# RWKV decay, rate and key scalings on ScalarE, and the last mLSTM block normalised on VectorE

## The chip, the cores and the metric

The kernel runs on one core of one Trainium2 chip. The metric is the device time of one execution in microseconds (us). Before the change it is 2755.69 us, the median of three runs (2754.13 to 2758.62 us). Engines are named as in the profile: PE is TensorE's matmuls, PEld its weight loads, DVE is VectorE, ACT is ScalarE, POOL is GpSimd, SP issues DMAs.

## What is computed

One layer over 4096 tokens of width 1024, batch 1, float32. One input projection feeds four mixers of width 256 (RWKV-7, multi-scale pooling, mLSTM, retention); each mixer's output is multiplied by a SiLU gate; the four are concatenated, projected, added to the residual and to a gated embedding, and layer-normalised. The parts that the change touches, cut from the reference:

```python
# RWKV: decay, rate and key
w_log = -jax.nn.softplus(-(w0 + jnp.tanh(wl) @ w2)) - 0.5
decay = jnp.exp(-jnp.exp(w_log))
a = jax.nn.sigmoid(a0 + al @ a2)
kk = normalised per head (k * k_k)
k = heads(k) * (1.0 + (a - 1.0) * k_a)
# state = state * decay + (state @ -kk) (kk * a)^T + v k^T ; y = state @ r
...
# mLSTM, at its end
h = num / jnp.maximum(jnp.abs(den), jnp.exp(-m_t))[..., None]
h = h * jax.nn.sigmoid(o_pre)
h = _head_norm(h, HEAD_NORM_EPS) * ln_w          # then times silu(gate)
```

`_head_norm` subtracts the mean over a head's 64 channels and divides by the standard deviation. The sigmoids are computed as tanh of half the argument, so that an affine step follows each tanh: for the decay it is `-0.5*exp(-0.5)*(t + 1)`, whose running sum over a chunk of 64 tokens goes into two exponentials; for the rate it is `-0.5*(t + 1)`; for the key it is `t * half[4+p] + half[6+p]`, a factor and an offset per channel.

## The kernel before, in words

The sequence is cut into 16 blocks of 256 tokens (`TB`, `NB`). The kernel runs in stages, one after the other over all blocks: pooling, retention, mLSTM (`_mlstm`), RWKV (`_rwkv_out`), and the output projection (`out`). Every float32 matmul of a projection is written as three matmuls on a high and a low part of its operands (`fetch`, lines 87 to 89: ACT casts the high part, DVE or POOL subtracts to get the low part).

The program is written for a scheduler that orders each engine's instructions ahead of time with its own timing model: an engine's queue is fixed when the program is built, and each engine then works through its queue in order. Instructions inside `self.soon()` have a higher priority there. In the RWKV stage the order of TensorE is written by hand: `mm` and `dense_k` keep program order, and the strings `START`, `THIRD` and `ORDER` say in which order pieces of the stages run (a name, a block offset, and how many eighths of a projection).

**RWKV, one block.** `la` projects the low-rank part. `k`, `r`, `v` and `g` project key, receptance, value and gate into one of two PSUM banks (`MM = 2`, tag `mm`); `mixed` (lines 1361 to 1373) empties a bank: for each half p, ACT multiplies (line 1369), then DVE adds the shifted part (line 1370). Stage `l` makes decay and rate: eight matmuls into `lw` and `lA`; ACT tanh into `tw` (line 319) and `ta` (line 320), each in two halves; the affine step of `tw` on DVE over 512 columns (line 321); two scans on DVE (line 323), one for each half; then ACT's two exponentials `E` (line 327) and `Ei` (line 328). Stage `n` normalises the key. Stage `m` makes the operands of the recurrence: `km` from `ta` on DVE, one instruction for each half (line 368), times `k` (line 370); `ta` scaled on DVE (line 371), then times `k` (line 375); products with `E` and `Ei` give `BK` (lines 378, 379) and `AR` (lines 382, 385). `inv` and `iv` invert 64x64 triangles with many small DVE instructions on `nt` and `xs` (lines 505, 514, 530), go through HBM and back into `X`, and `pt`, `px`, `pu`, `py` finish the inverse on PE.

**The chain of states.** `chain` runs twelve pieces for each block, at the letters C of the order: four chunks with three pieces each. In a chunk PE multiplies the state `S` by `AR` into `ry`; ACT copies `R` (line 636); PE makes `sa`; ACT copies `SAV` (line 643); PE makes `ds`; DVE updates the state in four instructions (line 660); ACT copies `Y` (line 666). The next chunk's first matmul needs the new state. Of the order of a steady block, the middle reads:

```python
"... C r.0/2 C l.0 r.0/3 C n.0 r.0/4 C vt.1 r.0 m.0 C g.0/4 ..."
```

**mLSTM's normalisation.** `mix(b)` ends with `head_norm` (line 711 on) on `Y` of 128 x 512. Statistics (lines 718, 720) and the added epsilon (line 722) are DVE's, the power -0.5 is POOL's (line 723). With `scaled=True`, as mLSTM calls it for all blocks, DVE then computes minus mean times `rs` (line 727) and ACT applies scale and offset, one instruction of 64 columns for each of 8 groups (line 729). With `scaled=False`, as retention and RWKV call it, DVE subtracts the mean (line 732), which doesn't need the power, and multiplies by `rs` (line 733), over 512 columns each. After either, DVE multiplies by the gate (line 1301) and SP stores the block.

The last mLSTM block and the start of RWKV overlap: `rwkv_first` has projected block 0's `la`, `k`, `r` and gate, and `START` goes on with `v#0/3 l#0 v#0 n#0 m#0 la#1 k#1/4 ...`.

Of the kernel before, what the change touches and what calls it, by code (L numbers as in the profile page):

```python
# [9 lines left out]
F32 = mybir.dt.float32  # L10
F32R = mybir.dt.float32r
AF = mybir.ActivationFunctionType
ALU = mybir.AluOpType
# [4 lines left out]
P = 128  # L18
# [22 lines left out]
DECAY = math.exp(-0.5)  # L41
HEAD_EPS = 1e-6
# [4 lines left out]
class Trunk:  # L47
# [148 lines left out]
    def _rwkv_out(self, es):  # L196
        nc, tc, a = self.nc, self.tc, self.a
        pool = lambda name, **kw: es.enter_context(tc.tile_pool(name=name, reuse_waits="tile", **kw))
        cp = pool("rc", bufs=1)
        p1 = pool("r1", bufs=1)  # L200
# [8 lines left out]
        V = nc.vector  # L209
        A = nc.scalar  # L210
        Q = nc.gpsimd
# [12 lines left out]
        smask = self.load(cp, "smask")  # L224
        lnw = self.load(cp, "rw_ln_w", a["rw_ln_w"].partition_broadcast(P))
        lnb = self.load(cp, "rw_ln_b", a["rw_ln_b"].partition_broadcast(P))
        half = cp.tile([P, 8], F32, name="rhalf", tag="rhalf")
        V.tensor_scalar(out=half[:, 0:4], in0=prm[:, 7:11], scalar1=0.5, scalar2=None, op0=ALU.mult)
        V.tensor_scalar(out=half[:, 4:6], in0=prm[:, 13:15], scalar1=0.5, scalar2=None, op0=ALU.mult)
        V.tensor_scalar(out=half[:, 6:8], in0=half[:, 4:6], scalar1=-1.0, scalar2=1.0, op0=ALU.mult, op1=ALU.add)  # L230
# [66 lines left out]
        @stage  # L297
        def l(b):

            la = bl[b]["la"]  # L300
            lah = p1.tile([P, 2, TB], F32R, name=f"lah{b}", tag="E")
            lal = p1.tile([P, 2, TB], F32R, name=f"lal{b}", tag="ta")
            lz = [wk.tile([P, 2, TB], F32, name=f"l{g}{b}", tag="wk") for g in range(2)]
            for g in range(2):
                own, other = slice(64 * g, 64 * g + 64), slice(64 - 64 * g, 128 - 64 * g)
                A.copy(out=lah[own, g], in_=la[own])
                A.copy(out=lah[other, g], in_=la[own])
                Q.memset(lal[other, g].bitcast(F32), 0.0)
                V.tensor_tensor(out=lal[own, g], in0=la[own], in1=lah[own, g].bitcast(F32), op=ALU.subtract)
            for g in range(2):  # L310
                for p in range(2):
                    mm(lz[g][:, p], LW[g][:, p], lah[:, g], start=(p == 0), stop=False, skip_group_check=True)
                for p in range(2):
                    mm(lz[g][:, p], LW[g][:, p], lal[:, g], start=False, stop=(p == 1), skip_group_check=True)
            lw, lA = lz
            tw = p1.tile([P, 2, TB], F32, name=f"tw{b}", tag="tw")
            ta = p1.tile([P, 2, TB], F32, name=f"ta{b}", tag="ta")
            for p in range(2):
                A.activation(out=tw[:, p], in_=lw[:, p], func=AF.Tanh, scale=0.5, bias=half[:, p:p + 1])
                A.activation(out=ta[:, p], in_=lA[:, p], func=AF.Tanh, scale=0.5, bias=half[:, 2 + p:3 + p])  # L320
            V.tensor_scalar(out=tw, in0=tw, scalar1=-0.5 * DECAY, scalar2=-0.5 * DECAY, op0=ALU.mult, op1=ALU.add)
            for p in range(2):
                V.tensor_tensor_scan(out=tw[:, p], data0=smask, data1=tw[:, p], initial=0.0, op0=ALU.mult, op1=ALU.add)
            E = p1.tile([P, 2, 4, 65], F32, name=f"E{b}", tag="E")
            Ei = t4(tw)
            Q.memset(E[:, :, :, 0:1], 1.0)
            A.activation(out=E[:, :, :, 1:], in_=Ei, func=AF.Exp)
            A.activation(out=Ei, in_=Ei, func=AF.Exp, scale=-1.0)
            eC = p2.tile([P, 2, 4], F32, name=f"eC{b}", tag="eC", bufs=3)
            Q.tensor_copy(out=eC, in_=E[:, :, :, 64])  # L330
            bl[b].update(ta=ta, E=E, Ei=Ei, eC=eC)
            yield 0.9
# [30 lines left out]
        @stage  # L363
        def m(b):
            k, r, ta, E, Ei = (bl[b][x] for x in ("k", "r", "ta", "E", "Ei"))
            km = p1.tile([P, 2, TB], F32, name=f"km{b}", tag="km")
            for p in range(2):
                V.tensor_scalar(out=km[:, p], in0=ta[:, p], scalar1=half[:, 4 + p:5 + p], scalar2=half[:, 6 + p:7 + p],
                                op0=ALU.mult, op1=ALU.add)
            V.tensor_tensor(out=km, in0=km, in1=k, op=ALU.mult)  # L370
            V.tensor_scalar(out=ta, in0=ta, scalar1=-0.5, scalar2=-0.5, op0=ALU.mult, op1=ALU.add)
            BK = p1.tile([P, 2, 2, 4, 64], F32, name=f"BK{b}", tag="BK")
            AR = [p4.tile([P, 2, 4, 64], F32, name=f"AR{b}_{cc}", tag="AR") for cc in range(2)]
            for p in range(2):
                V.scalar_tensor_tensor(out=ta[:, p], in0=k[:, p], scalar=prm[:, 11 + p:12 + p], in1=ta[:, p],
                                       op0=ALU.mult, op1=ALU.mult)
            for cc in range(2):
                V.tensor_tensor(out=BK[:, :, cc, 0::3], in0=c5(t4(km))[:, :, cc], in1=c5(Ei)[:, :, cc], op=ALU.mult)
                V.tensor_tensor(out=BK[:, :, cc, 1:3], in0=c5(t4(ta))[:, :, cc], in1=c5(Ei)[:, :, cc], op=ALU.mult)
            for cc in range(2):  # L380
                for p in range(2):
                    V.scalar_tensor_tensor(out=AR[cc][:, p, 1:3], in0=c5(t4(k))[:, p, cc],
                                           scalar=prm[:, 11 + p:12 + p], in1=c5(E[:, :, :, 0:64])[:, p, cc],
                                           op0=ALU.mult, op1=ALU.mult)
                V.tensor_tensor(out=AR[cc][:, :, 0::3], in0=c5(t4(r))[:, :, cc], in1=c5(E[:, :, :, 1:])[:, :, cc],
                                op=ALU.mult)
            rk = p1.tile([P, 2, TB], F32, name=f"rk{b}", tag="tw")
            Q.tensor_tensor(out=rk, in0=r, in1=km, op=ALU.mult)
            ST = [p4.tile([P, 2, 2, P], F32, name=f"ST{b}_{cc}", tag="ST") for cc in range(2)]
            g1 = [p4.tile([P, 2, 2, 2, P], F32, name=f"g1{b}_{cc}", tag="g1") for cc in range(2)]  # L390
            bl[b].update(rk=rk, BK=BK, AR=AR, ST=ST, g1=g1)
            return
            yield
# [296 lines left out]
        for i in range(self.NB + 2):  # L690
            gens = {}
            for w in ("" if i == 1 else START if i == 0 else THIRD if i == 2 else ORDER).split():
# [6 lines left out]
                nm, b = w.replace("#", ".").split(".")  # L699
                b = int(b) if "#" in w else i - int(b)  # L700
# [376 lines left out]
    def _mlstm(self, es):  # L1077
# [5 lines left out]
        cp = pool("mc", bufs=1)  # L1083
        self.mm = pool("mmm", bufs=3, space=PSUM)
        ident = self.ident
        V, A, Q = nc.vector, nc.scalar, nc.gpsimd
# [128 lines left out]
        def mix(b):  # L1215
# [28 lines left out]
            Y = p2.tile([P, 2, G], F32, name=f"Ym{b}", tag="Ym")  # L1244
            tot = p2.tile([P, 2, 4, 65], F32, name=f"tot{b}", tag="tot", bufs=1)
            for c in range(2):
# [40 lines left out]
                for i in range(4):  # L1287
# [9 lines left out]
                            in0=tot[:, :, :, 0:64].rearrange("p c h v -> p (c h) v"),  # L1297
                            in1=den.rearrange("p c h -> p (c h)").unsqueeze(2).broadcast_to([P, 8, 64]), op=ALU.mult)
            V.scalar_tensor_tensor(out=Y, in0=so, scalar=1.0, in1=Y, op0=ALU.add, op1=ALU.mult)
            self.head_norm(p1, Y, HEAD_EPS, f"m{b}", True)  # L1300
            V.scalar_tensor_tensor(out=Y, in0=Y, scalar=0.5, in1=sg, op0=ALU.mult, op1=ALU.mult)
            self.store(b, 2, Y)

# [2 lines left out]
        p1 = pool("m1", bufs=1)  # L1306
        p2 = pool("m2", bufs=2)
        wk = pool("mwk", bufs=1, space=PSUM)
        for i in range(1, self.NB + 1):
            if i < self.NB:  # L1310
                dense(i)
            mix(i - 1)
# [483 lines left out]
```

## Time and profile before

| | before |
|---|---|
| median of three runs | 2755.69 us |
| profiled execution, device time | 2756.33 us |
| profiled execution, span of the trace | 2754.5 us |
| mLSTM's last normalisation and RWKV's start | about 1207 to 1300 us of the span |
| RWKV, steady blocks | about 1300 to 1840 us |
| RWKV, last blocks, with the first embedding blocks | about 1840 to 2020 us |

The span is the time from the first to the last instruction in the profile; the 1.8 us between it and the execution's time lie around it. Times in the rows are counted from the start of the span. A matmul's busy time is modelled, and matmuls overlap in the pipeline, so a stretch in which PE is shown as fully busy can still hold short waits: those are read from the idle times, not from the share.

### The profile page before, as it was taken

The page shows a single profiled execution, that of the slowest core. Times are in us where ns is not written, and L with a number is a line of the kernel's source. Part 1 is how long each engine was busy: PE and PEld are TensorE (multiplying, and loading weights), DVE is VectorE, ACT ScalarE, POOL GpSimd, SP SyncE. Part 2 cuts the span into 40 slices and gives each one's busy share as a digit, 9 for nine tenths or more (in the row PEclk, how much of TensorE's full clock was granted, in tenths as well). Part 3 has the DMA queues.
Part 4 walks back from the last instruction along what each step waited for, and adds up shares of the span by engine and source line. Part 5 has one row for each costly group of instructions (what it writes and reads, how often), then busy time and mean ns, then how long its engine had stood idle before and what let it go on. Part 6 is the DMA issues. An engine that isn't in the chain of part 4 may idle for free.

```text
span 2754.5 us, 57727 instructions
## 1 busy us (share of the span) xinstructions
PE 2653.0 (96%) x21940; PEld 2382.7 (87%) x21940; DVE 2142.6 (78%) x5241; ACT 1111.2 (40%) x2700; POOL 1142.9 (41%) x1302
## 2 busy tenths in 40 slices
PE   8999999998999999989999999999989999899996
PEld 8998888878899999988999999998988888778885
DVE  6767888886887777777888888888564666789997
ACT  4323222334666666653444444445222333422221
POOL 4664555554433434431323333324243111266665
PEclk9999999999999999999999999999999999999998
DMA  5453222223311112231111111113366444734431
GB/s 170 146 174 113 59 61 66 66 69 95 99 55 58 55 55 65 74 107 34 53 39 51 39 51 39 51 40 110 117 197 220 135 140 145 237 123 156 157 138 69
DMA packets 251909, 270.66 MB, mean 98 GB/s; under 512 B 69616, under 2 KB 175344, under 8 KB 251632
## 3 DMA queue, kind: packets, MB, share of 16 engines
q1 hardware_dynamic: 251632, 266.98, 31.0%
q8 instruction: 172, 2.82, 0.4%
q14 instruction: 105, 0.86, 0.1%
HBM read 203.40 MB, written 63.50 MB: 97 GB/s over the span
## 4 chain that ended last, share of the span: by engine, by line
PE 40%; DVE 16%; DMA 7%; issue 4%; POOL 3%; ACT 2%; SPq 1%; POOLq 0%; DVEq 0%; ACTq 0%
PE ry L262 2%; DVE ro L1688 2%; PE zqk L150 2%; PE zqk L151 2%; PE zqk L149 2%; DVE nt L505 1%; DVE ro L1667 1%; DVE ro L1670 1%; PE zg L158 1%; DMA nd<-g 1%; POOL ro L1671 1%; PE zg L159 1%; PE zg L160 1%; DVE so L1662 1%; PE num L1265 1%
## 5 line engine op out<-in xcount | busy, mean ns | idle before, releaser
L1446 ACT CAST Ah<-xr 128x512 fp32r<-128x512 f32 x189 | 117.0, 620 | 280.7 <-PE zrb L1482 55.3
L1447 DVE TENSOR_TENSOR Al<-xr,Ah 128x512 fp32r<-128x512 f32 x135 | 95.6, 710 | 80.6 <-ACT Ah L1446 77.2
L150 PE MATMUL zqk<-xl,wh_w_ml 128*128 128x256 f32 x512 | 150.6, 294 | 0.8 <-DVE xl L1126 0.8
L149 PE MATMUL zqk<-xh,wh_w_ml 128*128 128x256 f32 x512 | 149.8, 293 | 1.5 <-ACT xh L1125 1.2
L88 ACT CAST xh<-rawx 128x512 fp32r<-128x512 f32 x148 | 91.5, 619 | 146.4 <-DMA rawx<-in_xT 65.9
L151 PE MATMUL zqk<-xh,wl_w_ml 128*128 128x256 f32 x512 | 148.5, 290 | 0.0
L89 DVE TENSOR_TENSOR xl<-rawx,xh 128x512 fp32r<-128x512 f32 x148 | 116.0, 784 | 28.5 <-ACT xh L88 27.5
L677 POOL TENSOR_TENSOR SAV<-SAV,bon 64x256 f32<-64x256 f32 x64 | 42.9, 671 | 227.2 <-PE ry L262 226.1
L1447 POOL TENSOR_TENSOR Al<-xr,Ah 128x512 fp32r<-128x512 f32 x54 | 71.0, 1314 | 139.7 <-ACT Ah L1446 75.3
L1671 POOL TENSOR_TENSOR ro<-ro,ln_b 128x512 f32<-128x512 f32 x64 | 100.7, 1593 | 53.9 <-DVE ro L1670 53.9
L912 POOL TENSOR_TENSOR rot<-rot,sw 128x256 f32<-128x256 f32 x64 | 69.2, 1082 | 95.4 <-DVE sw L911 89.5
L149 PEld LDWEIGHTS zqk<-xh,wh_w_ml 128*128 128x128 f32 x512 | 99.1, 194 | 3.2 <-ACT xh L1125 1.5
L150 PEld LDWEIGHTS zqk<-xl,wh_w_ml 128*128 128x128 f32 x512 | 99.4, 194 | 2.9 <-DVE xl L1126 1.0
L151 PEld LDWEIGHTS zqk<-xh,wl_w_ml 128*128 128x128 f32 x512 | 99.3, 194 | 0.8
L1466 POOL TENSOR_TENSOR xr<-xr,xr 128x512 f32<-128x512 f32 x27 | 35.6, 1317 | 143.0 <-DVE xr L1463 132.7
L660 DVE SCALAR_TENSOR_TENSOR S<-ds,eC,Se 64x64 f32<-64x64 f32 x256 | 72.4, 283 | 22.0 <-PE ds L262 17.0
L1237 DVE SCALAR_TENSOR_TENSOR xc<-zc,c_convw,xc 128x256 f32<-128x256 f32 x192 | 83.3, 485 | 0.4
L437 DVE SCALAR_TENSOR_TENSOR g<-gp,rc,c_rmask 128x128 f32<-128x128 f32 x256 | 69.0, 341 | 18.3 <-PE gp L262 17.2
L149 PE MATMUL zu<-xh,wh_w_pl 128*128 128x256 f32 x256 | 74.8, 292 | 6.1 <-ACT wh_w_pl L88 6.1
L657 POOL TENSOR_TENSOR Se<-S,eC 64x128 f32<-64x128 f32 x128 | 59.2, 463 | 48.8 <-DVE S L660 44.0
L150 PE MATMUL zu<-xl,wh_w_pl 128*128 128x256 f32 x256 | 73.8, 288 | 3.9 <-DVE xl L89 3.9
L1446 ACT CAST Aho<-s 128x512 fp32r<-128x512 f32 x48 | 29.7, 621 | 115.3 <-PE zob L1482 52.4
(1130 smaller groups left out, 10570.2 us busy)
## 6 DMA issues: line engine op xcount, KB each, us to landing
rawx<-in_xT SPq DMA_DIRECT2D x148, 256.0 KB, 3.2
xr<-in_xT SPq DMA_DIRECT2D x108, 256.0 KB, 2.9
mr<-in_xT SPq DMA_DIRECT2D x64, 256.0 KB, 3.1
rp<-in_x SPq DMA_DIRECT2D x64, 256.0 KB, 3.0
s<-rp SPq DMA_DIRECT2D x64, 256.0 KB, 2.7
yo<-y SPq DMA_DIRECT2D x16, 1024.0 KB, 4.9
ro<-s SPq DMA_DIRECT2D x16, 1024.0 KB, 5.0
out<-ro SPq DMA_DIRECT2D x32, 512.0 KB, 2.6
```

The costliest lines, as they stand in the source:

```text
L88: nc.scalar.copy(out=hi, in_=raw)
L89: eng.tensor_tensor(out=lo, in0=raw, in1=hi.bitcast(F32), op=ALU.subtract)
L149: nc.tensor.matmul(out, lh(k), rh(k), start=(k == 0 and (apart or i == 0)), stop=False, skip_group_check=True)
L150: nc.tensor.matmul(out, lh(k), rl(k), start=False, stop=False, skip_group_check=True)
L151: nc.tensor.matmul(out, ll(k), rh(k), start=False, stop=(k == nk - 1), skip_group_check=True)
L437: V.scalar_tensor_tensor(out=g1[cc][:, hh, p, e], in0=gp[hh][:, p, e], scalar=rc[:, cc, e, i:i + 1], in1=msk[:, 64 * e:64 * e + P], op0=AL ...
L660: V.scalar_tensor_tensor(out=Sn[hv, p, hv], in0=ds[hv, p], scalar=eC[hv, p, c:c + 1], in1=Se[hv, p], op0=ALU.mult, op1=ALU.add)
L912: Q.tensor_tensor(out=r3, in0=r3, in1=sw, op=ALU.add)
L1237: V.scalar_tensor_tensor(out=xc[:, t], in0=zc[t // 2][:, t % 2, j:j + TB], scalar=cw[:, t, j:j + 1], in1=xc[:, t], op0=ALU.mult, op1=ALU.add)
L1446: self.nc.scalar.copy(out=hi, in_=src)
L1447: eng.tensor_tensor(out=lo, in0=src, in1=hi.bitcast(F32), op=ALU.subtract)
L1671: Q.tensor_tensor(out=rg, in0=rg, in1=ln["ln_b", g], op=ALU.add)
```

## The change

In RWKV, four instructions of each block move from DVE to ACT, as Identity activations with a scale and a bias: the affine step of `tw`, both halves of `km`, and the affine step of `ta`. Two constants for them are written by POOL into two new columns of `half`, once. In mLSTM, `head_norm` is called with `scaled` false for the last block (b = 15) and true for the others.

```diff
-        half = cp.tile([P, 8], F32, name="rhalf", tag="rhalf")
+        half = cp.tile([P, 10], F32, name="rhalf", tag="rhalf")
+        Q.memset(half[:, 8:9], -0.5)
+        Q.memset(half[:, 9:10], -0.5 * DECAY)
...
-            V.tensor_scalar(out=tw, in0=tw, scalar1=-0.5 * DECAY, scalar2=-0.5 * DECAY, op0=ALU.mult, op1=ALU.add)
+            A.activation(out=tw, in_=tw, func=AF.Identity, scale=-0.5 * DECAY, bias=half[:, 9:10])
...
             for p in range(2):
-                V.tensor_scalar(out=km[:, p], in0=ta[:, p], scalar1=half[:, 4 + p:5 + p], scalar2=half[:, 6 + p:7 + p],
-                                op0=ALU.mult, op1=ALU.add)
+                A.activation(out=km[:, p], in_=ta[:, p], func=AF.Identity, scale=half[:, 4 + p:5 + p],
+                             bias=half[:, 6 + p:7 + p])
             V.tensor_tensor(out=km, in0=km, in1=k, op=ALU.mult)
-            V.tensor_scalar(out=ta, in0=ta, scalar1=-0.5, scalar2=-0.5, op0=ALU.mult, op1=ALU.add)
+            A.activation(out=ta, in_=ta, func=AF.Identity, scale=-0.5, bias=half[:, 8:9])
...
-            self.head_norm(p1, Y, HEAD_EPS, f"m{b}", True)
+            self.head_norm(p1, Y, HEAD_EPS, f"m{b}", b + 1 < self.NB)
```

## Rows read from the trace of the kernel before

**Rows 1.** The page: each engine's busy time, share of the span, instructions.

```profile
PE 2653.0 (96%) x21940; PEld 2382.7 (87%) x21940; DVE 2142.6 (78%) x5241; ACT 1111.2 (40%) x2700; POOL 1142.9 (41%) x1302
```

**Rows 2.** Busy time by stretch: length, PE, PEld, DVE, ACT, POOL, granted clock, DMA.

```profile
1300.00:1840.00 540.00, 535.12 (x7590) 502.99 (x7589) 463.28 (x1460) 231.52 (x605) 175.83 (x298) 1.00 0.17 45
...
1214.50:1222.00 7.50, 1.53 (x10) 0.93 (x8) 7.27 (x21) 3.87 (x11) 3.10 (x6) 0.85 0.32 105
...
1220.00:1225.00 5.00, 3.04 (x14) 3.04 (x15) 4.67 (x14) 2.04 (x5) 1.64 (x3) 0.50 0.09 31
...
1242.40:1259.30 16.90, 15.62 (x154) 14.77 (x152) 16.06 (x50) 6.43 (x16) 3.75 (x6) 1.00 0.16 50
```

**Rows 3.** Waits of TensorE's weight loads, 1195 to 1300 us: us, times, longest.

```profile
PEld z1k L158 <- DVE v L1370: 3.9, 1, 3.9
```

**Rows 4.** The same, 1300 to 1840 us.

```profile
PEld ry L262 <- DVE S L660: 6.7, 18, 0.5
PEld sa L262 <- ACT R L636: 3.1, 11, 0.4
```

**Rows 5.** Instructions of one line: count, least, median and largest duration (ns).

```profile
L321 DVE TENSOR_SCALAR tw<-tw x16: 406/414/427, 1209.9 to 1883.2; 128x512 f32<-128x512 f32 x16
...
L368 DVE TENSOR_SCALAR km<-ta,rhalf x32: 395/404/408, 1213.8 to 1889.3; 128x256 f32<-128x256 f32 x32
...
L328 ACT ACTIVATE tw<-tw x16: 623/630/633, 1216.7 to 1886.9; 128x512 f32<-128x512 f32 x16
...
L340 ACT ACTIVATE sq<-k,c_prm x32: 492/506/522, 1203.6 to 1883.9; 128x256 f32<-128x256 f32 x32
...
L732 DVE TENSOR_TENSOR Y<-Y,mvr x16: 677/682/685, 1318.2 to 2008.7; 128x512 f32<-128x512 f32 x16
```

**Rows 6.** VectorE in order of time at RWKV's start: start, us, instruction, idle before.

```profile
1211.90 0.17 DVE L727 SCALAR_TENSOR_TENSOR mvm<-mvm,rsm 128x8 f32<-128x8 f32 x1 [1.53 <-POOL rsm L723]
1211.99 1.27 DVE L323 TENSOR_TENSOR_SCAN tw<-c_smask,tw 128x256 f32<-128x256 f32 x2
...
1214.90 0.69 DVE L1301 SCALAR_TENSOR_TENSOR Ym<-Ym,sgm 128x512 f32<-128x512 f32 x1 [0.23 <-ACT Ym L729]
...
1217.26 0.47 DVE L1370 SCALAR_TENSOR_TENSOR v<-z0v,c_prm,v 128x255 f32<-128x255 f32 x1
...
1221.44 0.47 DVE L1370 SCALAR_TENSOR_TENSOR v<-z0v,c_prm,v 128x255 f32<-128x255 f32 x1
```

**Rows 7.** ScalarE in order of time, the same stretch.

```profile
1212.11 2.76 ACT L729 ACTIVATE Ym<-Ym,mvm,rsm 128x64 f32<-128x64 f32 x8 [2.68 <-DVE mvm L727]
...
1215.85 0.47 ACT L1369 ACTIVATE v<-z0v,omu 128x256 f32<-128x256 f32 x1
```

**Rows 8.** VectorE in order of time, in a steady block.

```profile
1518.34 0.42 DVE L321 TENSOR_SCALAR tw<-tw 128x512 f32<-128x512 f32 x1
...
1519.00 1.42 DVE L323 TENSOR_TENSOR_SCAN tw<-c_smask,tw 128x256 f32<-128x256 f32 x2
1520.34 0.58 DVE L505 TENSOR_TENSOR nt<-xs,nt 64x256 f32<-64x256 f32 x1
1520.85 1.20 DVE L660 SCALAR_TENSOR_TENSOR S<-ds,eC,Se 64x64 f32<-64x64 f32 x4
```

**Rows 9.** TensorE's matmuls in order of time, in the same block.

```profile
1517.61 0.45 PE L262 MATMUL ds<-SAV,ST 128*64 128x64 f32 x8
...
1521.49 1.10 PE L262 MATMUL ry<-S,AR 128*128 128x128 f32 x4
```

**Rows 10.** ScalarE in order of time, in the same block.

```profile
1518.02 0.83 ACT L320 ACTIVATE ta<-l,rhalf 128x256 f32<-128x256 f32 x2
1518.88 0.37 ACT L666 COPY Y<-ry 64x256 f32<-64x256 f32 x1
1520.45 0.63 ACT L327 ACTIVATE E<-tw 128x512 f32<-128x512 f32 x1 [1.21 <-DVE tw L323]
...
1522.63 0.37 ACT L636 COPY R<-ry 64x256 f32<-64x256 f32 x1 [0.33 <-PE ry L262]
```

## Prediction, made before the changed kernel had run

> **What bounds the kernel now.** The page comes first: TensorE is busy for 96% of the span, VectorE for 78%, ScalarE for 40% [rows 1]. That is a mean over five stages, and the change lies in one of them and at its border, so the next view is busy time by stretch. In RWKV's steady blocks, 540 us and twelve blocks, TensorE is busy for 535 us, VectorE for 463 us (86%), ScalarE for 232 us (43%) [rows 2]. TensorE's order sets the pace there, and moving work between the other two pays only where TensorE waits for one of them. So the view of who waited for whom comes third. In the steady blocks two waits are left: `ry` on the state from VectorE, 6.7 us in 18 waits, and `sa` on `R` from ScalarE, 3.1 us in 11 [rows 4]. That 6.7 us is all that a faster VectorE can return there.
>
> At the start of RWKV the picture is another one. Between 1214.5 and 1222 us TensorE is busy for 1.53 of 7.5 us and VectorE for 7.27 [rows 2]: here VectorE is the bound. TensorE's weight load for `z1k` waits 3.9 us for line 1370's second half of `v` [rows 3], since that instruction empties the PSUM bank that `z1k` is to use. In order of time, ScalarE does the eight `Ym` instructions of the last mLSTM block from 1212.11 for 2.76 us, after 2.68 us idle, and reaches its first half of `v` at 1215.85 [rows 7]. VectorE runs line 1370 at 1217.26 and, behind other work, at 1221.44 [rows 6]. After this pause TensorE's granted clock is 0.50 between 1220 and 1225 us, the 1.2 GHz level, with 3.04 us of matmuls in it [rows 2]: at full clock these take about half, so the low clock costs 1.5 us.
>
> **The change part by part.**
>
> *Moved steps, by duration.* For each block VectorE loses line 321 (0.414 us), line 368 twice (0.404 us each), and line 371, of the same shape as line 321 and taken at its price: together 1.64 us [rows 5]. ScalarE has no Identity of these shapes. For 512 columns I take line 328, an activation from SBUF to SBUF, 0.63 us; for 256 columns line 340, the same with an operand per channel, 0.51 us [rows 5]. That is 2 x 0.63 + 2 x 0.51 = 2.3 us for each block. A second per-channel operand may add to it; below this it can't go much, as line 340's least is 0.49. Over the twelve steady blocks ScalarE goes from 43% to 48%, VectorE from 86% to 82%: neither becomes a bound by its sum, and the 27 us and 20 us cost or return nothing by themselves. What counts is where the steps stand in the two queues.
>
> *mLSTM's last block.* ScalarE loses 2.76 us [rows 7]. VectorE loses line 727 (0.17 us) and the 0.23 us of idle time before line 1301 [rows 6], and gains two instructions of 512 columns at 0.68 us [rows 5]. The first, the subtraction, needs no power from POOL, so it fits in the 1.53 us that VectorE idles for POOL [rows 6]. The multiplication waits for POOL as line 727 does now; behind it on VectorE stand the scans and the RWKV start, as now.
>
> *RWKV's start.* VectorE's work from 1211.90 to the end of `v` at 1221.91 is what TensorE waits for. Out of it go 0.17 and 0.23, both halves of line 368 (0.81) and line 371 (0.41): 1.62 us; in comes the multiplication, 0.68. The least gain is therefore 0.95 us. The 1.53 us of idle time and the place of line 321, 0.41, also take the subtraction (0.68) and the scans (1.27 us [rows 6]) if `tw` comes from ScalarE in time, and ScalarE idles for 2.68 us just there [rows 7]: then 2.2 us. The most is the whole wait, 3.9 us [rows 3], if the second half of `v` moves forward in VectorE's queue because ScalarE can begin it up to 2.76 us earlier, plus the 1.5 us of the low clock if the pause becomes short enough: 5.4 us. I take 3.8 us, halfway between 2.2 and 5.4, because the 2.76 us freed on ScalarE stand directly ahead of `v`. What is late next is x's low parts and the operands `BK` on the same VectorE queue, shortened likewise.
>
> *First inversion.* From 1242.4 to 1259.3 us VectorE is busy for 16.06 of 16.9 us [rows 2], and its last instruction there feeds the trip through HBM that the first `pt` waits for. Lines 368 and 371 lie in it: 1.2 us at most. Against it stands that `E`, and VectorE's work behind it, can come later because `tw` now waits for ScalarE: by 0.63 us less the 0.41 removed, or up to 0.9 us if other ScalarE work goes first. I take a gain of 0.8 us, between -0.9 and +1.2.
>
> *Steady blocks.* `ds`, the input of the state update, starts on TensorE at 1517.61; the update runs on VectorE at 1520.85 for 1.20 us, behind line 321 (1518.34), two scans (1519.00) and a piece of the inversion; the next `ry` starts at 1521.49 [rows 8, 9]. Without line 321 what stands ahead is 0.41 us shorter, 4.9 us in twelve blocks. But the scans now wait for ScalarE. Its `ta` ends at 1518.85 and the copy of `Y` follows at 1518.88 [rows 10]; a step of 0.63 us right behind `ta` ends near 1519.5, half a microsecond after the scans start now. If the update gets ahead of the scans in the queue, all 6.7 us can go; if it stays behind, the wait grows (below). I take a gain of 2.4 us, half of 4.9: ScalarE's 1.21 us of idle time ahead of `E` [rows 10] can take the step without delaying `R`. The ends are +6.7 and -10.8. The steps in stage m (lines 368, 371) precede products that TensorE uses pieces later, so I cost them at nothing; their cover is the rest of VectorE's queue in that piece, and if it is gone, `sa` waits for a later `R`, up to 0.63 us for each block.
>
> *The rest.* Two one-column writes on POOL, once, and two columns more in `half`: nothing, as POOL is a third busy and nothing on TensorE waits for it here [rows 2, 4]. The last RWKV blocks: taken as zero.
>
> **Sum.** 3.8 + 0.8 + 2.4 = 7.0 us. The profiled execution took 2756.33 us, 0.64 above the median of 2755.69; 2756.33 - 7.0 - 0.64 = 2748.7 us.
>
> **The rivals.**
>
> *Slower: the scans wait for ScalarE, and the state waits behind the scans.* For it speaks that each step is longer on ScalarE, 0.63 against 0.41 us [rows 5], and that line 319, line 321 and the scans are one chain. If the step is queued behind both `ta` and the copy of `Y`, it ends near 1519.9, 0.9 us after the scans start now; the update stays behind them, and TensorE, which waits for it already [rows 4, 9], waits 12 x 0.9 = 10.8 us more. Less 3.8 us from the start, that is 7.0 us slower: 2762.7 us. It decides from the point where the scans come later by (5.5 + 3.8) / 12 = 0.78 us. Against it: the update has a higher priority than the scans and can go first once they are late. The Trainium skill (ScalarE: Activation LUTs, Rules for kernel authors) says that multiplications and additions should stay on VectorE and not go to ScalarE, which would make this change a loss in every block. Chance 0.18.
>
> *No change: TensorE's order hides it all.* With 535 of 540 us busy [rows 2], the later scans may just eat line 321's 0.41 us, and the start give its least, 0.95 us: 2754.7 us. For it: the sums of both engines stay off the bound. Against it: the 3.9 us wait is real and VectorE is full there. Chance 0.25, and with it goes the case that the queues come out so that `v` is emptied no earlier.
>
> *A large gain.* The update overtakes the scans in each block, 6.7 us, the start gives 5.4 us and the inversion 1.2 us: 13.3 us, 2742.4 us. Chance 0.12.
>
> **How the numbers follow.** The forecast has 0.45, with its own range 2745 to 2752. About 0.2% (5.5 us) is what a measurement of this kernel can tell from no change; below 2750.2 us is faster. Of the forecast's 0.45 some 0.35 lies below it; with the large gain, 0.47 for faster. The other 0.10 and the no-change case make 0.35; 0.18 is slower. The range reaches from 2740 us, past the large gain, to 2760 us, which leaves out the worse half of the slower case.
>
> **What would show it.** Right: the pause of TensorE ahead of `z1k` shorter by 2 us or more, with the subtraction of line 732 inside VectorE's wait for POOL; `Ym` of the last block gone from ScalarE; the wait of `ry` on the state below 6.7 us in the twelve steady blocks. Wrong: that wait grown to 10 us or more with the scans released by ScalarE; `sa` waiting longer for `R`; a period of the steady blocks that is unchanged while VectorE's share falls to 82%. Most of all the forecast fails if the built order of the queues differs between the two kernels in places that the change doesn't touch, since all queues are ordered anew.

## The result, and the profile after

The changed kernel takes **2801.94 us** (median of five runs, 2792.27 to 2803.01); the kernel before took 2756.48 us beside it (five runs, 2754.13 to 2760.61). The ratio is 1.0155, with a 95% interval of 1.014 to 1.017: slower by 45 us, where 8 us faster was forecast, and outside the range.

The page of the kernel after, its engines (busy time, share of the span, instructions), to be read beside [rows 1]:

```profile
PE 2672.7 (95%) x21940; PEld 2406.3 (86%) x21940; DVE 2126.6 (76%) x5178; ACT 1143.0 (41%) x2756; POOL 1149.9 (41%) x1304
```

ScalarE gained 32 us and VectorE lost 16, each with the sign of the instructions that moved; TensorE's own busy time grew by 20 us with the same 21940 matmuls. That is the first sign of a lower clock. In the kernel after, line numbers behind line 227 are 2 higher than before; rows of an experiment have the lines of its own kernel.

To see where the 47 us lie (the two spans are 2801.2 and 2754.5 us), I cut the span at four matmuls: the first `z1k`, and the first `vt` of the fourth and of the fifteenth RWKV block, eleven blocks apart. Each entry is a difference of two start times in the order-of-time view, in us:

| kernel | start of `z1k` | `z1k` to fourth `vt` | eleven blocks | of one | rest |
|---|---|---|---|---|---|
| before | 1222.0 | 163.7 | 503.6 | 45.8 | 865.2 |
| after | 1223.1 | 163.9 | 551.8 | 50.2 | 862.4 |

So the steady blocks lost 48.2 us and nothing else moved by more than 3 us. The `z1k` of after is later only because this execution was already 2.9 us later at mLSTM's first `Ym` instruction, where nothing differs; counted from there it is 1.8 us earlier.

Busy time by stretch of the kernel after (length, PE, PEld, DVE, ACT, POOL, granted clock, DMA): the steady stretch of [rows 2], the start, and one block cut in three.

```profile
1300.00:1840.00 540.00, 505.67 (x6992) 478.98 (x6991) 422.58 (x1329) 239.62 (x607) 170.74 (x279) 0.96 0.16 42
...
1220.00:1225.00 5.00, 1.93 (x9) 1.93 (x10) 5.00 (x17) 2.87 (x8) 0.48 (x3) 0.70 0.30 104
1534.50:1539.00 4.50, 1.82 (x15) 1.55 (x14) 4.39 (x19) 2.71 (x7) 2.41 (x5) 1.00 0.24 31
1539.00:1545.80 6.80, 6.13 (x44) 6.02 (x45) 3.97 (x11) 2.81 (x8) 1.96 (x4) 0.53 0.11 30
1545.80:1582.00 36.20, 36.20 (x536) 34.45 (x535) 26.91 (x84) 13.18 (x35) 10.42 (x16) 0.99 0.18 47
```

The same 540 us now hold 6992 matmuls in place of 7590. Within a block there is a pause (1.82 us busy of 4.5), and behind it a stretch at 0.53 of the clock in the mean, close to the 1.2 GHz level, before the rest runs at full clock. The waits of TensorE's weight loads from 1300 to 1840 us (us, times, longest) name the pause, beside [rows 4]:

```profile
PEld sa L264 <- ACT R L638: 35.6, 11, 3.6
PEld ry L264 <- DVE S L662: 1.3, 2, 0.9
```

The wait on the state fell from 6.7 to 1.3 us. The one on `R` rose from 3.1 to 35.6, about 3.2 us for each block. One block in order of time shows why. VectorE first, then ScalarE, then TensorE (start, us, instruction, idle before):

```profile
1534.13 1.21 DVE L662 SCALAR_TENSOR_TENSOR S<-ds,eC,Se 64x64 f32<-64x64 f32 x4
1535.38 1.43 DVE L325 TENSOR_TENSOR_SCAN tw<-c_smask,tw 128x256 f32<-128x256 f32 x2
```

```profile
1532.89 0.73 ACT L323 ACTIVATE tw<-tw,rhalf 128x512 f32<-128x512 f32 x1
...
1534.04 1.09 ACT L370 ACTIVATE km<-ta,rhalf 128x256 f32<-128x256 f32 x2
1536.90 0.63 ACT L329 ACTIVATE E<-tw 128x512 f32<-128x512 f32 x1 [1.76 <-DVE tw L325]
1537.44 0.71 ACT L373 ACTIVATE ta<-ta,rhalf 128x512 f32<-128x512 f32 x1
1538.05 0.61 ACT L330 ACTIVATE tw<-tw 128x512 f32<-128x512 f32 x1
...
1538.74 0.48 ACT L1371 ACTIVATE r<-z7r,omu 128x256 f32<-128x256 f32 x1
1539.25 0.37 ACT L638 COPY R<-ry 64x256 f32<-64x256 f32 x1
```

```profile
1535.17 0.71 PE L264 MATMUL ry<-S,AR 128*128 128x128 f32 x4
...
1539.67 0.79 PE L264 MATMUL sa<-R,X 64*64 64x64 f32 x5 [3.35 <-ACT R L638]
```

The built order of VectorE's queue has turned round: before, the scans came first and the state update after them [rows 8]; now the update is first. So `ry` starts early and ends at 1535.88. But ScalarE's queue still has `E` ahead of `R`, `E` needs the scans, and the scans are now late: ScalarE idles until 1536.90 and then does `E`, the moved step of `ta`, `Ei`, the copy `zl` and `r` before it reaches `R` at 1539.25. Counted from `ry`'s end, that is 1.02 us until `E`, 0.54 from `E` to `ta`, 0.61 from `ta` to `Ei` and 1.20 from there to `R`, 3.37 in all, against the 3.35 us that `sa` waits. Before, all of these were over when `ry` ended, and `R` waited for `ry` [rows 10].

The scans were late because of the update ahead of them, and not because of ScalarE: in this block the moved step of `tw` ended at 1533.62 (1532.89 + 0.73), and the scans started 1.76 us later, straight behind the update.

### The profile page after: what moved, and what is told of

Same layout as the page of the kernel before. It is cut to its first block, busy times and chain, and to the rows that moved or that the text cites. A ratio compares the mean times of both kernels' runs of the same rounds, so it can differ in the third digit from the quotient of the medians.

```text
span 2801.2 us, 57749 instructions
## 1 busy us (share of the span) xinstructions
PE 2672.7 (95%) x21940; PEld 2406.3 (86%) x21940; DVE 2126.6 (76%) x5178; ACT 1143.0 (41%) x2756; POOL 1149.9 (41%) x1304
## 4 chain that ended last, share of the span: by engine, by line
PE 39%; DVE 18%; DMA 5%; issue 4%; POOL 3%; ACT 3%; SPq 1%; POOLq 0%; DVEq 0%; ACTq 0%
DVE ro L1690 2%; DVE nt L507 2%; PE zqk L150 2%; PE zqk L151 2%; PE zqk L149 2%; PE ry L264 2%; DVE ro L1669 1%; DMA nd<-g 1%; PE zg L158 1%; DVE ro L1672 1%; PE zpl L149 1%; PE zpl L151 1%; PE zg L159 1%; PE zg L160 1%; PE zpl L150 1%
## 5 line engine op out<-in xcount | busy, mean ns | idle before, releaser
L1468 POOL TENSOR_TENSOR xr<-xr,xr 128x512 f32<-128x512 f32 x27 | 35.6, 1319 | 143.1 <-DVE xr L1465 143.1
L659 POOL TENSOR_TENSOR Se<-S,eC 64x128 f32<-64x128 f32 x128 | 67.9, 530 | 58.0 <-DVE S L662 53.3
L264 PE MATMUL sa<-R,X 64*64 64x64 f32 x512 | 46.0, 233 | 38.1 <-ACT R L638 38.1
L158 PE MATMUL zg<-wh_w_rw,xh 128*128 128x256 f32 x240 | 79.5, 331 | 0.0
```

What stands on the lines that cost most here:

```text
L158: keep(nc.tensor.matmul(out, lh(k), rh(k), start=(k == 0 and i == 0), stop=False, skip_group_check=True))
L264: mm = lambda *args, **kw: keep(nc.tensor.matmul(*args, **kw))
```

## The experiments

**Three parts, each by itself, and the whole with one order changed.** The first two have only some of the moved steps on ScalarE, and the normalisation of before; theory Q is that the order of the queues around `R` costs the time, rival L that the length of the steps on ScalarE does.

**e1_tw_only:** of the whole change, this alone.

```diff
-            V.tensor_scalar(out=tw, in0=tw, scalar1=-0.5 * DECAY, scalar2=-0.5 * DECAY, op0=ALU.mult, op1=ALU.add)
+            A.activation(out=tw, in_=tw, func=AF.Identity, scale=-0.5 * DECAY, bias=half[:, 9:10])
```

> Of the change only the decay step tw is on ScalarE; km, ta and the last normalisation are as before. Theory Q (queue order): moving tw alone makes the state update stand ahead of the scans, the exponential E then waits for the scans at the head of ScalarE's queue and R stands behind it; nearly the whole loss is there: steady blocks of 48 to 50 us against 45.7, the wait of sa on R 25 us or more over 1390 to 1890 us, 2785 to 2805 us. Rival L (load): ScalarE's added time ahead of R is what counts; tw is 0.73 of the 2.5 us added to each block, so about a third of the loss, 2765 to 2775 us.

Measured: 2798.68 us (2794.53 to 2801.43) against 2755.07 for before, ratio 1.0153 (1.0138 to 1.0168). In its profile the update stands ahead of the scans, `sa` waits 32.4 us for `R`, and eleven blocks take 548.0 us. One instruction of 0.73 us that moves is nearly the whole loss, as Q says.

**e2_kmta_only:** `km` and `ta` on ScalarE, `tw` as before.

```diff
-                V.tensor_scalar(out=km[:, p], in0=ta[:, p], scalar1=half[:, 4 + p:5 + p], scalar2=half[:, 6 + p:7 + p],
-                                op0=ALU.mult, op1=ALU.add)
+                A.activation(out=km[:, p], in_=ta[:, p], func=AF.Identity, scale=half[:, 4 + p:5 + p],
+                             bias=half[:, 6 + p:7 + p])
...
-            V.tensor_scalar(out=ta, in0=ta, scalar1=-0.5, scalar2=-0.5, op0=ALU.mult, op1=ALU.add)
+            A.activation(out=ta, in_=ta, func=AF.Identity, scale=-0.5, bias=half[:, 8:9])
```

> Of the change only km and ta are on ScalarE; tw stays on VectorE, normalisation as before. Theory Q: the scans stay ahead of the state update, as in the kernel before; 2750 to 2762 us, steady blocks of 45.5 to 46.5 us. Rival L: 1.8 of the 2.5 us added to each block, two thirds of the loss, 2780 to 2792 us.

Measured: 2771.96 us (2769.23 to 2774.85), ratio 1.0057 (1.0042 to 1.0072): between the two expectations. The order on VectorE is that of before, and `ry` waits 6.7 us for the state, as before. But ScalarE has the moved steps between `E` and `R` (same view as above):

```profile
1524.15 0.64 ACT L329 ACTIVATE E<-tw 128x512 f32<-128x512 f32 x1 [1.14 <-DVE tw L325]
1524.69 1.08 ACT L370 ACTIVATE km<-ta,rhalf 128x256 f32<-128x256 f32 x2
1525.67 0.62 ACT L330 ACTIVATE tw<-tw 128x512 f32<-128x512 f32 x1
1526.20 0.71 ACT L373 ACTIVATE ta<-ta,rhalf 128x512 f32<-128x512 f32 x1
...
1527.49 0.37 ACT L638 COPY R<-ry 64x256 f32<-64x256 f32 x1
```

`sa` waits 14.4 us for `R` in eleven waits, 11.3 more than before: 1.0 us a block. The eleven blocks take 20.3 us more (523.9 against 503.6), so the waits are about half of it. The low clock is there too; the stretch of [rows 2] and one block of this kernel:

```profile
1300.00:1840.00 540.00, 524.39 (x7378) 493.44 (x7374) 435.21 (x1381) 238.27 (x614) 169.34 (x286) 0.97 0.17 44
1428.50:1476.40 47.90, 46.31 (x637) 43.53 (x637) 37.97 (x121) 20.89 (x55) 14.58 (x25) 0.96 0.17 43
```

The granted clock is 0.97 over the stretch, in place of 1.00 before. So length does cost where the step stands ahead of the critical copy. It doesn't add to the cost of the `tw` step: in the block of the whole change shown above, `km` fits into ScalarE's idle time ahead of `E`, and only `ta` stands in the chain. The other side of these steps is the inversion: from `z1k` to the first `pt` is 42.7 us, where before has 44.8.

**e3_norm_only:** mLSTM's last block alone.

```diff
-            self.head_norm(p1, Y, HEAD_EPS, f"m{b}", True)
+            self.head_norm(p1, Y, HEAD_EPS, f"m{b}", b + 1 < self.NB)
```

> Of the change only the normalisation of the last mLSTM block on VectorE. Both theories: no loss; the pause ahead of z1k is 1 to 3 us shorter and the time 2751 to 2756 us, so faster by 0 to 0.2%.

Measured: 2758.32 us (2754.64 to 2763.21, ten runs), ratio 1.0013 (1.0002 to 1.0024). No gain in the time, where 0 to 0.2% was expected: a miss. In the profile the start does gain a little: `z1k` starts 11.33 us behind VectorE's added epsilon of that last block, before 12.08. But one of the eleven blocks takes 49.2 us, with a stretch at half clock from 1777.8 us on; whether other executions of this kernel have it isn't known.

**e4_r_ahead_of_E:** the whole change, with the two exponentials moved from stage `l` to stage `m` and issued behind `R`.

```diff
+            with tc.issue_after(state["R"].ins) if "R" in state else ExitStack():
+                A.activation(out=E[:, :, :, 1:], in_=Ei, func=AF.Exp)
+                A.activation(out=Ei, in_=Ei, func=AF.Exp, scale=-1.0)
```

> The changed kernel whole, with one thing more: the two exponentials of a block are issued behind the copy R that TensorE waits for, in ScalarE's queue. Theory Q: the wait of sa on R falls from 36 us to under 8 us and the low clock of the steady blocks goes with it; 2742 to 2758 us. Rival L: ScalarE has the same work in each block, so the loss stays, 2785 us or more.

Measured: 2760.45 us (2756.22 to 2767.78), ratio 1.0016 (1.0003 to 1.0028). With every moved step still on ScalarE, 40 of the 45 us are gone, though the time is 2.5 us above Q's range. The waits of 1300 to 1840 us:

```profile
PEld ry L264 <- ACT SAV L465: 8.1, 22, 0.6
PEld sa L264 <- ACT R L640: 7.8, 11, 0.9
```

`E` now stands ahead of the copies of `SAV`, and a part of the wait goes there.

**The order alone.** **e5_scans_last** is the kernel before, with no step moved; the scans and the exponentials go from stage `l` to stage `n`, and the scans are issued behind the state update.

```diff
+            with tc.issue_after(state["S"].ins) if "S" in state else ExitStack():
+                for p in range(2):
+                    V.tensor_tensor_scan(out=tw[:, p], data0=smask, data1=tw[:, p], initial=0.0, op0=ALU.mult, op1=ALU.add)
```

> The kernel before, with nothing moved to ScalarE; only the scans, and the exponentials after them, are issued behind the state update in VectorE's queue, as the changed kernel has them. Theory Q (queue order): E comes some 2 us later, R stands behind it, sa waits 2 to 3 us in each steady block and the clock falls: steady blocks of 47.5 to 49 us, 2775 to 2795 us. Rival L (ScalarE's load): no work is added to ScalarE, so no loss; 2745 to 2758 us.

Measured: 2799.13 us (2793.26 to 2805.98) against 2753.88 for before, ratio 1.0158 (1.0139 to 1.0177). The order alone costs what the whole change costs, 4 us more than the top of Q's range. VectorE, ScalarE and the wait in its profile:

```profile
1538.22 0.29 DVE L663 SCALAR_TENSOR_TENSOR S<-ds,eC,Se 64x64 f32<-64x64 f32 x1
1538.54 1.43 DVE L331 TENSOR_TENSOR_SCAN tw<-c_smask,tw 128x256 f32<-128x256 f32 x2
```

```profile
1540.00 0.63 ACT L335 ACTIVATE E<-tw 128x512 f32<-128x512 f32 x1 [3.44 <-DVE tw L331]
...
1541.87 0.37 ACT L639 COPY R<-ry 64x256 f32<-64x256 f32 x1
```

```profile
PEld sa L262 <- ACT R L639: 29.5, 11, 3.0
```

**e6_scans_first** is the other way round: the whole change, with the state update of the second chunk held behind the scans.

```diff
-                    for p, hh, hv in heads:
+                    with tc.issue_after(state["scan"].ins) if c == 1 and "scan" in state else ExitStack():
+                        for p, hh, hv in heads:
```

> The changed kernel whole, but the state update of the second chunk is issued behind the scans in VectorE's queue, as the kernel before has it. Theory Q: E and R come 1.3 us earlier, the state 1.3 us later, so that ry waits for the state again and sa for R less; part of the loss goes, 2768 to 2788 us. The slower rival of the prediction (state behind late scans) would be this kernel: 2763 us. Rival L: 2785 us or more.

Measured: 2771.85 us (2758.05 to 2774.95), ratio 1.0056 (1.0034 to 1.0078), as Q expected. `sa` waits 10.9 us for `R`, `ry` 9.8 us for the state. With the old order back the change costs as much as `km` and `ta` alone (2771.96 us).

**Can the order be made better than before's?** If the update goes first and nothing long stands ahead of `R`, both waits of [rows 4] should go. **e7_order_both** is the kernel before with the scans issued as in e5_scans_last and the exponentials as in e4_r_ahead_of_E.

> The kernel before, nothing moved to ScalarE, with both orders set: the scans behind the state update on VectorE, and the exponentials behind R on ScalarE. Theory Q: the waits of ry on the state (6.7 us) and of sa on R (3.1 us) of the kernel before go, nothing takes their place; 2743 to 2751 us. Rival T (TensorE's order hides it): within 3 us of the kernel before.

Measured: 2763.37 us (2758.56 to 2766.05), ratio 1.0034 (1.002 to 1.0047): slower, a miss. The waits of TensorE, and two neighbouring blocks:

```profile
PEld ry L262 <- ACT SAV L465: 11.3, 22, 1.0
PEld sa L262 <- ACT R L640: 3.7, 11, 0.4
...
PEld ry L262 <- DVE S L664: 0.3, 1, 0.3
```

```profile
1524.70:1570.50 45.80, 44.85 (x639) 42.41 (x638) 39.29 (x124) 19.58 (x52) 15.44 (x26) 1.00 0.17 45
1570.50:1617.80 47.30, 46.32 (x639) 43.85 (x638) 39.63 (x124) 19.39 (x52) 15.40 (x26) 0.96 0.16 44
1574.00:1577.40 3.40, 3.40 (x18) 3.40 (x17) 2.94 (x10) 1.17 (x3) 0.29 (x2) 0.50 0.26 77
```

The wait on the state is gone, and a wait for `SAV` of 11.3 us stands in its place: `E` is now between `R` and those copies. Both blocks have 639 matmuls; the second holds a stretch at half clock and takes 46.32 us of busy time in place of 44.85. So such a stretch costs 1.5 us by itself.

**e8_order_early_moves** is the same, with the steps of `km` and `ta` on ScalarE in the first three blocks alone (`if b < 3`).

> As e7_order_both, and km and ta on ScalarE for the first three blocks alone, where VectorE is the bound. Theory Q: the first pt comes 2 to 3 us earlier than in the kernel before, as in e2_kmta_only, and steady blocks are those of e7_order_both; 2 to 3 us below it. Rival: no different from e7_order_both, since the next wait takes it up.

Measured: 2754.62 us (2747.55 to 2765.71, twelve runs), ratio 1.0001 (0.9989 to 1.0013): level with before, 9 us below its partner. In the profiles, counted from VectorE's added epsilon of the last mLSTM block, the first `pt` comes 3.0 us earlier than its partner's (53.3 against 56.4 us), about what Q expected. Between 1300 and 1840 us its profile has two low-clock stretches, its partner's five, and its eleven blocks take 3.6 us less (509.8 against 513.4); why that differs stays open.

**Everything behind `SAV`.** In the last three kernels the exponentials wait for the chain's copy of `SAV` as well, and stage `m` stands one piece of the chain later in TensorE's order. **e9_order_behind_SAV** is the kernel before, with the scans behind the update as in e5_scans_last; **e10_order_and_early** has the early moves of e8_order_early_moves too; **e11_change_behind_SAV** is the whole change, its scans left as they are.

```diff
-ORDER = "C la.0 C k.0/2 C k.0 C r.0/2 C l.0 r.0/3 C n.0 r.0/4 C vt.1 r.0 m.0 C g.0/4 C g.0 v.0/2 C s0.0 v.0/1 pt.1 C p0.0 v.0/2 px.1 C bn.0 v.0/1 s1.0 v.0/2 pu.1 v.0/1 p1.0 v.0 py.1 inv.0 iv.0"
+ORDER = "C la.0 C k.0/2 C k.0 C r.0/2 C l.0 r.0/3 C n.0 r.0/4 C vt.1 r.0 C m.0 g.0/4 C g.0 v.0/2 C s0.0 v.0/1 pt.1 C p0.0 v.0/2 px.1 C bn.0 v.0/1 s1.0 v.0/2 pu.1 v.0/1 p1.0 v.0 py.1 inv.0 iv.0"
...
+            with tc.issue_after(state["SAV"].ins) if "SAV" in state else ExitStack():
+                A.activation(out=E[:, :, :, 1:], in_=Ei, func=AF.Exp)
+                A.activation(out=Ei, in_=Ei, func=AF.Exp, scale=-1.0)
```

> The kernel before with none of its steps moved. VectorE's scans are issued behind the state update, and ScalarE's exponentials E and Ei behind the copy of SAV in the eighth piece of the chain; stage m stands one piece later in the order of TensorE. In the run with the scans behind the update and the exponentials behind R, the waits of TensorE on the state and on R were nearly gone, but a new one of 11.3 us on the copy of SAV stood there. Theory Q (the order of the queues at the critical copies sets the block): with E behind that copy as well none of the three waits is left, the granted clock stays whole in most blocks, the period is about 45 us, and the time is 2742 to 2752. Rival N (TensorE's own queue, or the next late operand, takes up what a wait gives back): a wait of similar size appears elsewhere, behind the later E, and the time is within 3 us of before.

Measured: 2745.09 us (2742.42 to 2751.35) against 2755.37 for before, ratio 0.9969 (0.9957 to 0.998): faster than both kernels, within Q's expectation. Its waits, and one block:

```profile
PEld sa L262 <- ACT R L640: 4.0, 12, 0.4
PEld ry L262 <- ACT SAV L465: 2.4, 12, 0.2
```

```profile
1518.20:1562.90 44.70, 44.62 (x639) 42.28 (x637) 39.87 (x127) 19.36 (x52) 16.38 (x27) 1.00 0.17 47
```

Of the three waits that on the state is gone and that on `SAV` small, while that on `R` stays (Q had all three going). What is listed here is 6.4 us in twelve blocks, 0.5 us a block, so little is left to gain from the order in these blocks.

> The kernel of e9_order_behind_SAV, with the steps of km and ta on ScalarE for the first three RWKV blocks only. In e8_order_early_moves the first pt came 3 us earlier with these moves. Theory Q: 2 to 3 us below e9_order_behind_SAV, 2739 to 2750, a version that beats both kernels. Rival N: the same as e9_order_behind_SAV within 1 us, since what the start gives is waited for later.

Measured: 2746.33 us (2739.0 to 2752.13, twelve runs), ratio 0.9968 (0.9957 to 0.9979): no different from e9_order_behind_SAV, so the 2 to 3 us of Q aren't in the time. In the profile the early gain is there: the first `pt` comes 3.5 us earlier, counted from the same epsilon (53.6 against 57.1). But its eleven blocks take 4.1 us more (499.9 against 495.8), as one of them takes 49.2 us, with this in it, behind a wait of 1.6 us for the operand `ST`:

```profile
1720.00:1726.80 6.80, 6.80 (x67) 6.51 (x64) 6.15 (x16) 1.56 (x4) 3.29 (x4) 0.50 0.25 80
```

One profile can't say how often such a block occurs.

> The whole change, with the exponentials E and Ei issued behind the copy of SAV in the eighth piece and stage m one piece later. Theory Q: the pause of 3.3 us at sa goes in every block and with it the low clock behind it; the period is about 45 to 46 us and the time 2745 to 2760, at or below before. Rival L (the length of the moved steps on ScalarE costs by itself, 2.5 us for each block): 2770 to 2785 whatever the order.

Measured: 2745.84 us (2744.16 to 2750.67, twelve runs), ratio 0.9971 (0.9962 to 0.998). This settles it against L, which had 2770 us or more whatever the order: the same steps on ScalarE, with the queue mended, take 9.5 us less than before in place of 45 more. Its wait on `R` and one block:

```profile
PEld sa L264 <- ACT R L640: 9.0, 12, 0.9
```

```profile
1514.50:1559.70 45.20, 44.61 (x639) 42.25 (x638) 38.05 (x120) 21.76 (x56) 14.67 (x26) 1.00 0.18 46
```

Against the kernel without the moved steps a block is half a microsecond longer and `sa` waits 5 us more, which is 5.7 us in the eleven blocks. The start gives 2.8 us of that back: the fourth `vt` stands 171.7 us behind the epsilon of mLSTM's last block, there 174.5. The medians differ by 0.75 us, less than the runs of either scatter. With this order the change is worth nothing that can be told; the order of the queues decides.

The eleven blocks again, from the same two matmuls, for those on which the argument rests:

| kernel | eleven blocks | time |
|---|---|---|
| `tw` step alone | 548.0 | 2798.68 |
| `km` and `ta` alone | 523.9 | 2771.96 |
| before, scans last | 543.2 | 2799.13 |
| whole change, `R` ahead of `E` | 513.3 | 2760.45 |
| before, `E` behind `SAV` | 495.8 | 2745.09 |
| whole change, `E` behind `SAV` | 501.5 | 2745.84 |

## Why the prediction was wrong, step by step

**What bounds the kernel: right.** TensorE's order does set the pace in the steady blocks, and its two small waits were the place to look. Their 6.7 us can be had, and were, in the kernel with `E` behind `SAV`, but not by a faster VectorE.

**The steady blocks: the step that failed.** It said that "ScalarE's 1.21 us of idle time ahead of `E` [rows 10] can take the step without delaying `R`", and that "if the update gets ahead of the scans in the queue, all 6.7 us can go". The update did get ahead, and 5.4 of the 6.7 us went. What the step left out is the instruction behind the waiting one: ScalarE works in order, so an `E` that waits for late scans holds `R`, and with it `sa`, however free ScalarE is in the mean. The Trainium skill (Perfetto Trace Analysis, Tensor Engine Instruction (MATMUL, LD_WEIGHTS)) says in its notes that VectorE and ScalarE take their instructions strictly first in, first out; the trace agrees, with `ry` done at 1535.88, `R` at 1539.25, and `E` in front. The step also took it that the scans "now wait for ScalarE"; in the block above they waited for the update, with `tw` ready 1.76 us before. Of the prediction's signs of being wrong, "`sa` waiting longer for `R`" is the one that came; one of its signs of being right, a wait of `ry` below 6.7 us, came as well and told nothing of the time. In place of a gain of 2.4 us, or of the low end of -10.8, for twelve blocks, the profile shows -48.2 for eleven. The two blocks of the changed kernel that I read for this,

```profile
1535.70:1586.20 50.50, 47.15 (x638) 44.90 (x637) 38.07 (x120) 21.69 (x55) 15.38 (x26) 0.93 0.16 41
1586.20:1635.50 49.30, 45.95 (x639) 43.59 (x639) 39.28 (x122) 21.73 (x55) 16.28 (x27) 0.97 0.17 43
```

have 3.35 us each in which TensorE isn't busy, and 2.5 and 1.3 us more busy time than the 44.61 us that the same matmuls take at full clock in the last kernel above. Against the 45.8 us of before, that is 50.5 - 45.8 = 4.7 and 49.3 - 45.8 = 3.5 us; the mean over eleven blocks is 4.4. So the pause makes up 3.35 us of a block's loss and the low clock behind it 1.3 to 2.5, less the 1.2 us (45.8 - 44.6) by which a block of before is longer than 44.6 itself; the waits of [rows 4] are 0.8 us of that. The low clock was no term of the sum at all, though the prediction had priced it for the start.

**The steps in stage m: costed at nothing, wrongly.** Their cover was named as "the rest of VectorE's queue in that piece", with up to 0.63 us a block if it was gone. Alone they cost 1.0 us a block in waits and, with the low clock that stands beside these, 16.9 us in all. Here too the question was what stands behind them on ScalarE.

**The durations: too low.** 0.63 and 0.51 us were taken; measured are, least, median and largest in ns:

```profile
L323 ACT ACTIVATE tw<-tw,rhalf x16: 715/731/738, 1211.8 to 1932.4; 128x512 f32<-128x512 f32 x16
```

```profile
L370 ACT ACTIVATE km<-ta,rhalf x32: 585/596/617, 1219.8 to 1935.2; 128x256 f32<-128x256 f32 x32
```

```profile
L373 ACT ACTIVATE ta<-ta,rhalf x16: 705/706/723, 1221.2 to 1937.4; 128x512 f32<-128x512 f32 x16
```

Together 0.73 + 2 x 0.60 + 0.71 = 2.6 us a block in place of 2.3. An error of this size isn't the cause: the same durations stand in the kernel that beats before.

**The start: half of 3.8 us, and not as forecast.** `Ym` left ScalarE, as the prediction's list of signs had it. To see what `z1k` gained, it is best counted from VectorE's added epsilon of that mLSTM block, which stands just ahead of the moved instructions in VectorE's queue. Before, and then after:

```profile
1209.88 0.16 DVE L722 TENSOR_SCALAR rsm<-mvm 128x8 f32<-128x8 f32 x1
1221.96 0.58 PE L158 MATMUL z1k<-xh,wh_w_rw 128*128 128x256 f32 x1 [3.71 <-DVE v L1370]
```

```profile
1212.87 0.17 DVE L724 TENSOR_SCALAR rsm<-mvm 128x8 f32<-128x8 f32 x1
1223.07 0.58 PE L158 MATMUL z1k<-xh,wh_w_rw 128*128 128x256 f32 x1 [3.09 <-DVE v L1372]
```

That is 12.08 and 10.20 us, a gain of 1.9 us. The three kernels in which only the order is changed have 12.09 or 12.10, the three others with the whole change 10.20 or 10.21, so the gain is clear of what profiles scatter: above the least of 0.95 us, near the 2.2, and half of what was taken. VectorE's queue shows where it stopped (start, us, instruction, idle before), beside [rows 6]:

```profile
1212.94 0.68 DVE L734 TENSOR_TENSOR Ym<-Ym,mvm 128x512 f32<-128x512 f32 x1
1215.16 0.69 DVE L735 TENSOR_TENSOR Ym<-Ym,rsm 128x512 f32<-128x512 f32 x1 [1.54 <-POOL rsm L725]
...
1216.50 1.27 DVE L325 TENSOR_TENSOR_SCAN tw<-c_smask,tw 128x256 f32<-128x256 f32 x2
...
1222.54 0.47 DVE L1372 SCALAR_TENSOR_TENSOR v<-z0v,c_prm,v 128x255 f32<-128x255 f32 x1
```

The subtraction stands ahead of POOL's power as forecast, but it didn't use up the 1.53 us of idle time there: 1.54 us are left behind it, and the multiplication starts 2.29 us behind the epsilon, where line 727 started 2.02 behind it. The scans still stand behind the multiplication, and `E` with them, so the 2.76 us that `Ym` freed on ScalarE became idle time. ScalarE, and then the wait of TensorE's weight load from 1195 to 1300 us:

```profile
1217.86 0.63 ACT L329 ACTIVATE E<-tw 128x512 f32<-128x512 f32 x1 [4.28 <-DVE tw L325]
```

```profile
PEld z1k L158 <- DVE v L1372: 3.3, 1, 3.3
```

The wait is 0.6 us shorter than before [rows 3], far from the 2 us named as a sign, and the clock is low behind it again: 0.70 in the mean of 1220 to 1225 us.

**The first inversion: 0.8 us, measured 0.1.** From `z1k` to the first `pt` it is 44.7 us against 44.8. The parts are larger: `km` and `ta` alone give 2.1 us there, and `tw` alone loses 3.3 (48.1 us).

**POOL's two writes and the tail: nothing, as said.** The rest of the span is 2.8 us shorter; in the profiles of the other kernels it lies between 860.3 and 868.2 us, so this says nothing.

**The rivals.** "Slower" had the sign and the wrong mechanism: in it the state waited behind late scans, where in fact `R` did, behind an `E` that waited for the scans. Made to happen, its order costs 9.8 us of wait on the state in place of 6.7, where 10.8 more were forecast, and its time of 2771.85 us is that of the steps of stage m alone. "A large gain" had the event, the overtaking, and the wrong sign. Beside the "slower" case the prediction set the rule of the Trainium skill (ScalarE: Activation LUTs, Rules for kernel authors) that additions and multiplications stay on VectorE. The durations agree with it, 0.73 us against 0.41 [rows 5]; the time doesn't hang on it, since with the same steps on ScalarE 2745.84 us are reached. The prediction ended with the sentence that it fails most of all "if the built order of the queues differs", and that is what happened, at a place that the prediction had named, the update ahead of the scans. It had priced that event as a gain alone; the price of an `E` ahead of `R` was missing.

What makes the built order turn round when one step of 0.73 us moves was not tried on its own. That the scheduler sees the scans later and lets the update, with its higher priority, go first fits the prediction's remark, but is only argued.

## What to carry to other kernels

When an operation moves to another engine, follow its consumers to the next engine's queue and ask what stands behind each of them there: an in-order queue makes an idle engine's late instruction as costly as a busy engine. Where a scheduler orders the queues, price both orders before believing a gain from either, and pin the order around the critical copies: this was worth 9 to 10 us here with the steps moved or not, but only once the exponentials stood behind the copies of `SAV` too; one copy earlier, behind `R` alone, the time was 5 us above before's with the steps moved and 9 us above it without. To measure a gain of 1 or 2 us in profiles, count from a near instruction that the change doesn't reach. And a pause of TensorE has a second price behind it, at the lower clock, which the view of waits doesn't show.

## What the runs showed of the hardware

The low clock followed the 3.35 us pause in the block cut above: 0.53 from 1539.00 to 1545.80, after 1.82 us of matmuls in the 4.5 us before. In e7_order_both it also fell, five times between 1300 and 1840 us, though no wait listed there was longer than 1.0 us, and in e8_order_early_moves, with waits of the same lengths, twice; in e9_order_behind_SAV and e11_change_behind_SAV, with none above 0.9, it didn't fall there. What sets the five blocks apart from the others stays open. Where it fell, a block of as many matmuls took 1.5 us longer.

On ScalarE an Identity with a bias per channel takes 0.71 to 0.73 us for 512 columns, while an exponential of the same shape without one takes 0.63 [rows 5]. The Trainium skill (ScalarE: Activation LUTs, Rules for kernel authors) gives about 0.3 us and 0.83 ns per element for an activation with its bias as a pointer, an estimate of 0.72 us for 512; the trace agrees. The step of 256 columns has a scale per channel beside its bias, which that figure isn't for; it took 0.60 us.

POOL's power was not independent of VectorE's work. From the epsilon to the start of the instruction that needs the power it was 2.01 us in e1_tw_only, where VectorE has nothing between, 2.02 before, where it has the affine step of `tw` (0.42 us), 2.29 in the kernel after, with the subtraction (0.68 us), and 2.63 in e3_norm_only, with both. POOL's record of the power itself was 1.64, 1.66, 1.93 and 2.26 us. In the last three VectorE was idle for 1.53 to 1.54 us ahead of that instruction all the same. Why is not shown.
